# A two-layer hybrid encoder on one core: TensorE in the order in which the kernel emits its instructions

## The chip, the cores and the metric

The kernel runs on one NeuronCore of a Trainium2 chip. Its time is the device time of one execution in microseconds (us). Five engines work side by side, each through its own queue of instructions: TensorE (PE in the profile, with PEld for its weight loads), VectorE (DVE), ScalarE (ACT), GpSimd (POOL) and SyncE (SP), which issues nearly all DMA transfers. An instruction that waits holds up everything behind it on its engine.

## The reference, cut to what matters

Two layers work on 256 tokens of width 2048, all in float32. Each layer mixes (windowed attention with 8 heads beside a bidirectional mLSTM with 4 heads, both fed by one projection) and then runs an MLP:

```
h    = rms_norm(x, g_pre_mix)
proj = h @ w_in                       # 2048 -> 4624 columns
att  = window_attention(...)          # rope, |t-s| <= 128, a sink per head
mem  = mlstm_mixer(...)               # conv + silu on q/k, gates, forward and backward scans
x    = x + rms_norm(concat(att, mem) @ w_out, g_post_mix)
h    = rms_norm(x, g_pre_mlp)
u    = square(relu(h @ w_up))         # 2048 -> 8192
x    = x + rms_norm(u @ w_down, g_post_mlp)
```

## The kernel before, in words

**Weights and precision.** All weights come once, in pieces of up to 128 x 2048 values (1 MB). `load` (line 168) emits for each piece a DMA into `raw` (two buffers), a ScalarE copy to `whi` (line 191) and a VectorE subtraction to `wlo` (line 192), so that a value is a high and a low part. `whi` and `wlo` have four buffers each, and a copy may begin when TensorE has done its last matmul with the piece that held the buffer. Activations are split in the same way. Every product is three matmuls: high by high, high by low, low by high, in `mm_k` (lines 203 to 205) or in `mm_stationary` (lines 272 to 274).

**Tiles of a layer.** Ten `in` tiles of up to 512 columns (the fourth has 272), four `out` tiles, and four blocks of four `up` and four `down` tiles. In `mm_tile` (line 220) the activations are the loaded operand and a tile is 16 k steps by two halves of the tokens (t = 0, 1) by three matmuls, 96 in all. All up-tiles but a layer's first go through `mm_stationary`, where the weights are the loaded operand: 192 matmuls of 256 columns, in two pairs of two weight pieces. After each pair, `up_evac` applies Relu (line 848) and Square (849) on ScalarE to a tile `uz`, and then splits it into `uT`:

```
both = psmm.tile([P, 2, 512], F32, tag="mm", name="mms")
for pair in range(2):
    ps = both[:, pair].rearrange("p (i t) -> p i t", i=2)
    for i in range(2):
        hi, lo = pieces[key][2 * pair + i]
        ...
    after(pair, ps)
```

Results go to PSUM: pool `psmm` has two such tiles of two banks, pool `psax` four of one bank for everything else.

**Small work between the matmuls.** The attention and mLSTM work is written as generators. `mm_tile` calls `pump` (line 210) after each k step, which takes one step of the first generator in `urgent` and one in `later`. So the source itself interleaves six matmuls with a small step, and the generators hold yields (`SLACK`, three steps) between a producer and its consumer. The ones used below: `attend` (line 369: scores `sc`, probabilities `pr`, transposes `pp`, copy `pT`, product `po`), `side_kv` (transposes `pk`), `gates` (line 425: transposes `prow`, scans on VectorE, transposes `pcol` of `re`, `rwe` and `rb`), and `mlstm_head` (line 540: `st`, `dp`, `kp`, `cp`, `wp`, `pn`).

**Norms.** `pre` (line 327) makes a quarter of a normalized, transposed activation: four transposes `ptx` (line 332), a VectorE product `xg` (336), and a split into high (ScalarE, 324) and low part (325). The first tile of the program is fed in eight groups, each with its `pre` written directly ahead of its 12 matmuls. At the later boundaries `pre_at` (line 659) puts the calls between matmuls of the tiles before and after. The first up-tile ends in `up_first` (line 837: Relu, Square, transposes `ptu`).

**What sets the order.** The whole program is traced inside a tile context, whose scheduler simulates the engines. On each engine it takes the earliest-written instruction that its simulation holds to be ready, so an instruction written later may go ahead of one that has to wait. It also assigns buffers, and adds the waits. The change is in `kernel` (line 918).

## Time and profile before

| | |
|---|---|
| time, median of 3 runs | 2148.2 us (2144.47 to 2152.57) |
| the profiled execution's own time | 2145.2 us |
| its span, first to last instruction | 2143.4 us |
| mean granted TensorE clock | 0.996 of full speed |
| TensorE busy | 2100.0 us, 98% of the span |
| TensorE weight loads busy | 1855.3 us, 87% |
| VectorE busy | 1135.4 us, 53% |
| ScalarE busy | 983.9 us, 46% |
| GpSimd busy | 60.8 us, 3% |
| moved by DMA | 388.37 MB, mean 181 GB/s |

Matmuls are pipelined, so one lasts longer than the step from its start to the next one's. Where they follow each other without a wait, the step from start to start tells the pace. An engine's idle time matters only where it holds up the engine that has the most to do.

### The profile page before, as it was taken

To read this page: it belongs to the slowest core of one execution; us is meant where nothing else is said; L and a number is where in the kernel's file an instruction comes from. 1 tells how busy PE (TensorE), PEld (TensorE's weight loads), DVE (VectorE), ACT (ScalarE), POOL (GpSimd) and SP (SyncE) were. 2 spreads that over 40 slices of the span, in tenths; PEclk is the share of its full clock that TensorE was granted. 3 is DMA by queue.
4 is the path that set the end of the run, shared out by engine and by line. 5 is a ranking of instruction groups with operands and counts; after the bars stand their busy time and mean duration, and the time that the engine had idled before them with its cause. 6 is when DMAs were issued, how large, how long until landed. Compare 5 with 4: busy or idle time off the path is not lost.

```text
span 2143.4 us, 28980 instructions
## 1 busy us (share of the span) xinstructions
PE 2100.0 (98%) x12412; PEld 1855.3 (87%) x12412; DVE 1135.4 (53%) x1219; ACT 983.9 (46%) x1077; POOL 60.8 (3%) x68
## 2 busy tenths in 40 slices
PE   8999999999999999999999999999999999999998
PEld 6878887988998998898878788879889989989986
DVE  6656566544444444445567656464444444444454
ACT  5455545453443353345354555455445434533542
POOL 0000002000000000000020000030000000000000
PEclk9999999999999999999999999999999999999999
DMA  7434355555555455546444344545555555554553
GB/s 256 163 135 175 120 194 180 197 192 190 188 194 191 169 197 207 186 174 215 174 181 161 134 150 148 206 149 195 207 190 193 189 190 183 195 193 173 191 205 118
DMA packets 62209, 388.37 MB, mean 181 GB/s; under 512 B 9600, under 2 KB 10112, under 8 KB 17280
## 3 DMA queue, kind: packets, MB, share of 16 engines
q1 hardware_dynamic: 61936, 386.48, 51.4%
q8 instruction: 97, 1.59, 0.3%
q14 instruction: 32, 0.26, 0.0%
q10 hardware_dynamic: 144, 0.03, 0.0%
HBM read 384.39 MB, written 2.10 MB: 180 GB/s over the span
## 4 chain that ended last, share of the span: by engine, by line
PE 92%; DVE 2%; DMA 2%; ACT 2%; POOL 1%; issue 1%; SPq 1%; POOLq 0%; DVEq 0%; ACTq 0%
PE mm L205 19%; PE mm L204 19%; PE mm L203 19%; PE mms L272 10%; PE mms L274 10%; PE mms L273 10%; DMA raw<-wall 1%; PE sc L378 1%; PE pn L594 1%; DVE xs L792 1%; PE po L417 1%; DVE wlo L192 1%; POOL h2T L325 1%; ACT whi L191 0%; ACT uz L848 0%
## 5 line engine op out<-in xcount | busy, mean ns | idle before, releaser
L192 DVE TENSOR_TENSOR wlo<-raw,whi 128x2048 fp32r<-128x2048 f32 (+3 forms) x374 | 828.8, 2217 | 885.7 <-ACT whi L191 885.3
L191 ACT ACTIVATE whi<-raw 128x2048 fp32r<-128x2048 f32 (+3 forms) x374 | 693.9, 1855 | 922.7 <-PE mm L205 506.6
L272 PE MATMUL mms<-h2T,whi 128*128 128x256 f32 x1920 | 535.2, 279 | 7.0 <-ACT uz L848 6.8
L273 PE MATMUL mms<-h2T,whi 128*128 128x256 f32 x1920 | 533.3, 278 | 0.0
L274 PE MATMUL mms<-h2T,wlo 128*128 128x256 f32 x1920 | 530.5, 278 | 0.0
L204 PE MATMUL mm<-wlo,uT 128*128 128x512 f32 x1024 | 398.5, 389 | 0.0
L203 PE MATMUL mm<-whi,uT 128*128 128x512 f32 x1024 | 398.5, 389 | 0.0
L205 PE MATMUL mm<-whi,uT 128*128 128x512 f32 x1024 | 398.2, 389 | 0.0
L272 PEld LDWEIGHTS mms<-h2T,whi 128*128 128x128 f32 x1920 | 360.7, 188 | 11.8 <-ACT uz L848 11.1
L273 PEld LDWEIGHTS mms<-h2T,whi 128*128 128x128 f32 x1920 | 362.3, 189 | 0.3
L274 PEld LDWEIGHTS mms<-h2T,wlo 128*128 128x128 f32 x1920 | 360.0, 188 | 0.0
L203 PE MATMUL mm<-whi,hT 128*128 128x512 f32 (+2 forms) x640 | 241.9, 378 | 8.8 <-ACT hT L324 6.4
L205 PE MATMUL mm<-whi,hT 128*128 128x512 f32 (+2 forms) x640 | 241.7, 378 | 1.4 <-POOL hT L325 1.4
L204 PE MATMUL mm<-wlo,hT 128*128 128x512 f32 (+2 forms) x640 | 241.0, 377 | 0.0
L204 PEld LDWEIGHTS mm<-wlo,uT 128*128 128x128 f32 x1024 | 192.2, 188 | 39.7
L203 PEld LDWEIGHTS mm<-whi,uT 128*128 128x128 f32 x1024 | 192.2, 188 | 39.7
L205 PEld LDWEIGHTS mm<-whi,uT 128*128 128x128 f32 x1024 | 192.2, 188 | 39.4
L203 PEld LDWEIGHTS mm<-whi,hT 128*128 128x128 f32 x640 | 121.8, 190 | 29.0 <-ACT hT L324 7.0
L205 PEld LDWEIGHTS mm<-whi,hT 128*128 128x128 f32 x640 | 121.6, 190 | 22.7 <-POOL hT L325 2.2
L204 PEld LDWEIGHTS mm<-wlo,hT 128*128 128x128 f32 x640 | 121.7, 190 | 19.8
L869 DVE SCALAR_TENSOR_TENSOR A_mlp<-mm,s2q,A_mlp 128x512 f32<-128x512 f32 x48 | 34.0, 747 | 37.0 <-PE mm L205 37.0
L203 PE MATMUL mm<-whi,memT 128*128 128x512 f32 x128 | 50.5, 394 | 0.0
(221 smaller groups left out, 1460.5 us busy)
## 6 DMA issues: line engine op xcount, KB each, us to landing
raw<-wall SPq DMA_DIRECT2D x350, 1024.0 KB, 4.8
raw<-wall SPq DMA_DIRECT2D x8, 544.0 KB, 3.6
g<-gpost SPq DMA_DIRECT2D x16, 256.0 KB, 4.5
raw<-wall SPq DMA_DIRECT2D x8, 512.0 KB, 3.5
xs<-x_in SPq DMA_DIRECT2D x8, 256.0 KB, 5.2
raw<-wall SPq DMA_DIRECT2D x8, 256.0 KB, 6.1
y_out<-xs SPq DMA_DIRECT2D x8, 256.0 KB, 2.8
cossin<-rope SPq DMA_DIRECT2D x1, 256.0 KB, 7.1
```

The lines of the kernel that those rows point to most:

```text
L191: nc.scalar.activation(hi[:, sl], raw[:, sl], AF.Copy)
L192: nc.vector.tensor_tensor(out=lo[:, sl], in0=raw[:, sl], in1=hi[:, sl].bitcast(F32), op=ALU.subtract)
L203: nc.tensor.matmul(dst, lhsT=xh, rhs=hi, start=(k == 0), stop=False)
L204: nc.tensor.matmul(dst, lhsT=xh, rhs=lo, start=False, stop=False)
L205: nc.tensor.matmul(dst, lhsT=xl, rhs=hi, start=False, stop=(k == KC - 1))
L272: nc.tensor.matmul(ps[:, i], lhsT=hi[:, k], rhs=Tk[:, 0], start=(k == 0), stop=False)
L273: nc.tensor.matmul(ps[:, i], lhsT=hi[:, k], rhs=Tk[:, 1], start=False, stop=False)
L274: nc.tensor.matmul(ps[:, i], lhsT=lo[:, k], rhs=Tk[:, 0], start=False, stop=(k == KC - 1))
L325: (eng or nc.vector).tensor_tensor(out=lo, in0=ps, in1=hi.bitcast(F32), op=ALU.subtract)
L378: nc.tensor.matmul(sc[:, j], lhsT=qT[:, q0 + j, t * P:(t + 1) * P], rhs=kT[:, g], start=(j == 0), stop=False)
L417: nc.tensor.matmul(po[:, j], lhsT=vA[:, kb, g * HD:(g + 1) * HD], rhs=pT[:, kb], start=(kb == 0), stop=(kb == 1))
L869: nc.vector.scalar_tensor_tensor(out=acc[:, t, sl], in0=ps, scalar=s2[t], in1=acc[:, t, sl], op0=ALU.mult, op1=ALU.add)
```

## The change

TensorE is put under a manual schedule: its instructions keep the sequence in which the kernel's code emits them. VectorE, ScalarE, GpSimd and SyncE are still arranged by the scheduler, which simulates them against TensorE's fixed sequence. No instruction of the computation is added or removed.

```diff
     with tile.TileContext(nc, schedule_with_timeline_sim=True) as tc:
-        encoder_kernel(tc, *args)
+        with tc.manual_schedule(engines={mybir.EngineType.PE}):
+            encoder_kernel(tc, *args)
```

**Place one: the middle of a stationary up-tile, TensorE.** `mms` is the tile's PSUM, `h2T` the activations, `whi` and `wlo` the two parts of a weight piece. The names end in the numbers that the build gives them. Before, pair 0 of a tile (mms_3460) ends and the next tile (mms_3687) begins:

```order
L272 MATMUL mms_3460<-h2T1_2881,whi_3216 128x256
L273 MATMUL mms_3460<-h2T1_2881,whi_3216 128x256
L274 MATMUL mms_3460<-h2T1_2881,wlo_3217 128x256
L272 MATMUL mms_3687<-h2T0_2880,whi_3437 128x256 [waits Activation_49]
L273 MATMUL mms_3687<-h2T0_2880,whi_3437 128x256
L274 MATMUL mms_3687<-h2T0_2880,wlo_3438 128x256 [waits DVE_49]
```

and 41 matmuls later pair 1 of the first tile begins, after a wait for ScalarE:

```order
L274 MATMUL mms_3687<-h2T1_2881,wlo_3438 128x256
L272 MATMUL mms_3687<-h2T1_2881,whi_3437 128x256
L273 MATMUL mms_3687<-h2T1_2881,whi_3437 128x256
L272 MATMUL mms_3460<-h2T0_2880,whi_3222 128x256 [waits Activation_49]
L273 MATMUL mms_3460<-h2T0_2880,whi_3222 128x256
L274 MATMUL mms_3460<-h2T0_2880,wlo_3223 128x256
```

Now, at the same place (the tile is called mms_3462 here):

```order
L272 MATMUL mms_3462<-h2T1_2883,whi_3218 128x256
L273 MATMUL mms_3462<-h2T1_2883,whi_3218 128x256
L274 MATMUL mms_3462<-h2T1_2883,wlo_3219 128x256
L272 MATMUL mms_3462<-h2T0_2882,whi_3224 128x256 [waits Activation_49]
L273 MATMUL mms_3462<-h2T0_2882,whi_3224 128x256
L274 MATMUL mms_3462<-h2T0_2882,wlo_3225 128x256 [waits DVE_49]
```

Pair 1, whose first matmul waits for the Relu `uz` on pair 0, now follows pair 0 directly; the 41 matmuls of the next tile are behind it.

**The same place on ScalarE, now.** `raw` is a landed weight piece, `uz` the evacuated pair:

```order
L324 ACTIVATE uT0_2985<-uz_3433 128x2x256 [waits Activation_49]
L191 ACTIVATE whi_3439<-raw_3438 128x2048 [waits DMAHW3_49,DVE_49,PE_49]
L191 ACTIVATE whi_3445<-raw_3444 128x2048 [waits DMAHW4_49,DVE_49,PE_49]
L848 ACTIVATE uz_3559<-mms_3462 128x512 [waits PE_49,Pool_49]
L849 ACTIVATE uz_3559<-uz_3559 128x512 [waits Activation_49]
L324 ACTIVATE uT1_2986<-uz_3559 128x2x256 [waits Activation_49]
```

Before, the rows around this Relu are the same. The second of the two copies takes the buffer of the piece that pair 0 has just used. Its wait on PE is for the last-but-one matmul of pair 0, an L273, and the Relu's is for the last one, an L274.

**Place two: the start, TensorE.** `ptx` are the transposes of `pre`, `mm` the first tile. Before:

```order
L204 MATMUL mm<-wlo,hT_140 128x512
L205 MATMUL mm<-whi,hT_140 128x512
L332 MATMUL ptx<-ident,xs 128x128 x12
L203 MATMUL mm<-whi,hT_140 128x512
L204 MATMUL mm<-wlo,hT_140 128x512
L332 MATMUL ptx<-ident,xs 128x128
L205 MATMUL mm<-whi,hT_140 128x512
```

Now:

```order
L205 MATMUL mm<-whi,hT_142 128x512
L203 MATMUL mm<-whi,hT_142 128x512
L204 MATMUL mm<-wlo,hT_142 128x512
L205 MATMUL mm<-whi,hT_142 128x512
L332 MATMUL ptx<-ident,xs 128x128 x4
L203 MATMUL mm<-whi,hT_142 128x512
L204 MATMUL mm<-wlo,hT_142 128x512
```

The transposes of several groups went ahead together, between matmuls of earlier groups; now four stand directly ahead of the 12 matmuls that need them, eight times. On VectorE, the fourth to sixth group now (hT0 and hT1 are the low parts for k steps 0 to 7 and 8 to 15):

```order
L192 TENSOR_TENSOR wlo_188<-raw_184,whi_187 128x2048
L747 TENSOR_SCALAR nsink_8898<-snk_8896 128x8
L336 TENSOR_TENSOR xg_295<-ptx_290,gcol_96 128x512
L325 TENSOR_TENSOR hT0_142<-xg_295,hT0_142 128x4x128
L192 TENSOR_TENSOR wlo_203<-raw_201,whi_202 128x2048
L336 TENSOR_TENSOR xg_316<-ptx_311,gcol_96 128x512
L192 TENSOR_TENSOR wlo_209<-raw_207,whi_208 128x2048
L325 TENSOR_TENSOR hT1_143<-xg_316,hT1_143 128x4x128
L336 TENSOR_TENSOR xg_337<-ptx_332,gcol_96 128x512
```

Before, all eight `xg` stand ahead of the subtraction for the tile's fourth piece, so that of the weights only the third piece's lies among them; now five of them stand behind it or behind later ones.

**Place three: the gates, TensorE.** `pcol` holds transposes of `re`, `rwe` and `rb`, which VectorE and ScalarE make from `prow`. Before:

```order
L505 MATMUL pcol<-ident,re 128x36 x2
L535 MATMUL ptqk<-ident,qkn 128x128 x4
L203 MATMUL mm<-whi,hT_141 128x512
L204 MATMUL mm<-wlo,hT_141 128x512
L505 MATMUL pcol<-ident,rwe 128x36
L205 MATMUL mm<-whi,hT_141 128x512
```

Now:

```order
L205 MATMUL mm<-whi,hT_143 128x512
L505 MATMUL pcol<-ident,re 128x36 x2
L505 MATMUL pcol<-ident,rwe 128x36 x2
L505 MATMUL pcol<-ident,rb 128x36 x2
L203 MATMUL mm<-whi,hT_143 128x512
L204 MATMUL mm<-wlo,hT_143 128x512
```

The six transposes were spread over matmuls of the same tile and the next; now they stand together, 18 matmuls behind `prow`.

## Rows read from the trace of the kernel before

**Rows 1.** The page, part 1: engine, busy us (share of the span), instructions.

```profile
PE 2100.0 (98%) x12412; PEld 1855.3 (87%) x12412; DVE 1135.4 (53%) x1219; ACT 983.9 (46%) x1077; POOL 60.8 (3%) x68
```

**Rows 2.** Groups by line and form: count | busy us, mean ns | idle before, releasers.

```profile
L191 ACT ACTIVATE whi<-raw 128x2048 fp32r<-128x2048 f32 x350 | 671.6, 1919 | 888.0 <-PE mm L205 493.1 <-PE mms L273 255.4 <-DMA raw<-wall 118.9
```

**Rows 3.** Waits of TensorE: us in total, times, longest.

```profile
PE mms L272 <- ACT uz L848: 6.8, 15, 0.5
...
PE pp L411 <- DVE pr L400: 3.0, 4, 1.2
PE po L417 <- ACT pT L414: 2.8, 2, 2.1
```

**Rows 4.** Timeline of TensorE in up-tiles: start us, duration us, operation [idle before <-releaser].

```profile
611.40 0.39 PE L274 MATMUL mms<-h2T,wlo 128*128 128x256 f32 x2
611.62 0.28 PE L272 MATMUL mms<-h2T,whi 128*128 128x256 f32 x1
...
617.75 0.40 PE L203 MATMUL mm<-whi,uT 128*128 128x512 f32 x1
618.60 0.39 PE L272 MATMUL mms<-h2T,whi 128*128 128x256 f32 x1 [0.45 <-ACT uz L848]
```

**Rows 5.** Timeline of ScalarE, same place.

```profile
611.60 1.93 ACT L191 ACTIVATE whi<-raw 128x2048 fp32r<-128x2048 f32 x1 [3.51 <-PE mms L273]
613.43 0.58 ACT L848 ACTIVATE uz<-mms 128x512 f32<-128x512 f32 x1
...
617.95 0.60 ACT L848 ACTIVATE uz<-mms 128x512 f32<-128x512 f32 x1 [0.24 <-PE mms L274]
```

**Rows 6.** Stretches: us, busy (count) by engine, then PEclk, DMA share, GB/s.

```profile
133.70:137.00 3.30, 3.30 (x12) 2.67 (x10) 1.35 (x4) 0.81 (x2) 0.00 (x0) 0.50 0.55 179
140.50:143.90 3.40, 3.16 (x8) 2.49 (x9) 0.79 (x4) 0.18 (x1) 0.00 (x0) 0.50 0.00 0
...
372.50:376.00 3.50, 2.82 (x12) 2.01 (x12) 3.40 (x6) 2.30 (x5) 3.50 (x3) 1.00 0.00 0
...
1075.75:1079.10 3.35, 2.80 (x7) 2.22 (x8) 2.83 (x7) 3.35 (x6) 2.52 (x3) 0.50 0.68 248
```

**Rows 7.** Timeline of TensorE at three longer gaps.

```profile
132.25 0.70 PE L417 MATMUL po<-pT,scr 128*128 128x256 f32 x2 [2.10 <-ACT pT L414]
...
372.28 0.50 PE L203 MATMUL mm<-whi,h2T 128*128 128x512 f32 x1 [1.33 <-ACT h2T L324]
...
1074.87 0.50 PE L203 MATMUL mm<-whi,hT 128*128 128x512 f32 x1 [2.76 <-ACT hT L324]
```

**Rows 8.** Timeline of TensorE where tile 0 ends.

```profile
36.00 0.39 PE L204 MATMUL mm<-wlo,hT 128*128 128x512 f32 x1
36.23 0.39 PE L205 MATMUL mm<-whi,hT 128*128 128x512 f32 x1
38.52 0.41 PE L694 MATMUL pk<-ident,ra 128*128 128x128 f32 x2 [1.91 <-DVE ra L363]
```

**Rows 9.** Timeline of VectorE in tile 0.

```profile
14.60 0.69 DVE L336 TENSOR_TENSOR xg<-ptx,gcol 128x512 f32<-128x512 f32 x1
...
15.99 0.69 DVE L325 TENSOR_TENSOR hT<-xg,hT 128x512 fp32r<-128x512 f32 x1 [0.45 <-ACT hT L324]
...
27.88 2.29 DVE L192 TENSOR_TENSOR wlo<-raw,whi 128x2048 fp32r<-128x2048 f32 x1 [0.22 <-ACT whi L191]
...
34.77 2.29 DVE L192 TENSOR_TENSOR wlo<-raw,whi 128x2048 fp32r<-128x2048 f32 x1 [3.86 <-ACT whi L191]
```

**Rows 10.** Timelines of TensorE and ScalarE at the gates of layer 0.

```profile
153.72 0.60 PE L458 MATMUL prow<-ident,gpad 128*36 128x128 f32 x4
...
167.58 0.40 ACT L495 ACTIVATE rb<-rb 36x256 f32<-36x256 f32 x1
```

**Rows 11.** Timeline of VectorE at the first attention pair.

```profile
77.01 0.69 DVE L385 TENSOR_REDUCE mx<-sc 128x2 f32<-128x512 f32 x1 [0.83 <-PE sc L381]
...
79.53 0.62 DVE L400 TENSOR_SCALAR pr<-pr,rs 128x256 f32<-128x256 f32 x2
```

## The prediction

> **What bounds the kernel now.** I read the page's busy times first, then what TensorE waits for, then the timeline where it waits. TensorE is busy for 98% of a span of 2143.4 us [rows 1]. Its matmuls follow each other at a fixed pace, 0.23 us for 512 columns [rows 8] and 0.11 us for 256 columns [rows 4], so what is not pace is a wait for another engine. The view of waits puts the largest part of these, 6.8 us in 15 waits, between the stationary up-tiles and `uz`, the Relu that ScalarE applies to a finished pair, and finds 3.0 and 2.8 us at the attention's `pp` and `po` [rows 3]. So the kernel is a stream of TensorE instructions with almost nothing lost, and what the change can do is add waits or take these few away. Nearly all of that is settled by one question per place: how much TensorE work stands between a producer and its consumer, before and now.
>
> **Up-tiles, the main term.** A stationary tile is computed as two pairs, and the first matmul of pair 1 waits for the Relu on pair 0. Before, the scheduler put matmuls of the next tile in between: 41 of them in 14 of the 30 tiles, one or two in the other 16. Now nothing stands there, in all 30 (15 a layer). What ScalarE does at that point is the second half of the story: in its new sequence the copy `whi` of a weight piece stands directly ahead of the Relu in all 30 tiles, and that copy is released by the last-but-one matmul of the pair, so it always starts first. The trace of before shows this very sequence under its cover: the last matmul of a pair starts at 611.40, `whi` runs from 611.60, the Relu from 613.43 for 0.58, to 614.01 [rows 4, 5]. TensorE starts 0.05 us after a Relu ends (618.55 to 618.60 in the same rows). Uncovered, the next matmul starts at 614.06 instead of 611.51: 2.55 us lost, times 30 is **+77 us**. In exchange the short waits of before go: a matmul of 512 columns was followed after 0.85 us instead of 0.23 [rows 4], 0.62 us in about 15 places, **-9 us**. Bounds: if the Relu came first, a boundary would cost 0.58 plus the 0.2 between matmul and ScalarE's start, some 0.75 us, 22 us in all; if the piece's transfer were late as well, up to one more `whi` (1.92 us [rows 2]) each, 57 us more. I take the value of the trace, as its whole sequence is there.
>
> **The clock after such a stall.** After the idle 2.10 us at 130.1 and the 2.76 us at 1072.1, TensorE's granted clock stood at its lower level, 1.2 GHz, over stretches of 3.3 to 3.4 us [rows 6, 7]; after 1.33 us at 370.9 it stayed at 2.4 GHz [rows 6, 7]. A stretch of 3.4 us at half speed costs 1.7 us of matmuls. The new stalls leave TensorE idle for about 2.4 us (its last matmul ends 0.2 us into them), between the two that were followed by a slow stretch. Bounds 0 and 30 x 1.7 = 51 us; with two rows for it and one of half the length against it I take 18 of 30, **+31 us**. The Trainium skill's page "TensorE: Matmul & The Clock Gate" (section "Why this matters for your kernels") advises no idle gaps above about 3 us between bursts of matmuls. By that rule these stalls are short enough and this term is nothing, 31 us less in the sum; the trace's 2.10 us speaks against it.
>
> **Start of the program.** Tile 0 runs in eight groups (four pieces by two token tiles), each with its own four transposes `ptx`. Before, the scheduler sent the transposes of later groups ahead. Now a group's transposes come only after the group before it, and its matmuls wait for the whole chain `xg`, `hT`, low part: from 14.60 to 16.68, 2.1 us [rows 9]. Seven groups by 2 us are +14 us, the lower bound of this term. VectorE's new sequence makes it worse: it puts `xg` of the fourth, fifth and seventh groups behind (or their low part behind) a weight subtraction `wlo`. The fourth waits for the one at 27.88 and the fifth for those at 34.77 and after [rows 9]. With 2.29 us for a second `wlo`, the fifth group can run to its third matmul only at about 40.8 and ends at 43.3; three more of 5.3 us (0.4 transposes, 2.1 chain, 0.1, 2.7 matmuls) and one `wlo` in the seventh end tile 0 near 61.5, where before it ended at 36.2 [rows 8]: +25. The 1.91 us before `pk` go, since 24 matmuls now stand ahead of it [rows 8]. **+23 us**; the upper bound is +35, if the last four groups run at the lower clock.
>
> **Mixer stage, both layers.** `prow` to the last `pcol` is a long chain on VectorE and ScalarE: from 153.72 to 167.98, when ScalarE has finished `rb` [rows 10]. About half of those 14 us are weight copies and attention work in between. Before, some 70 matmuls covered it; now 18 do (4.1 us), and all three transposes stand together. **+8 us** (4 a layer; bounds 2 and 10 a layer). Attention: scores to probabilities take 3.1 us undisturbed [rows 11]; behind the second scores now stand 24 matmuls, 5.4 us, but 2.9 to 4.2 us where the 272-column tile runs, and one `whi` with its `wlo` (4.2 us) can come between. Between `pp` and `po` stand 6 matmuls, 1.4 or 0.7 us, for a copy of 0.6 us plus its start. I allow 2.5 us for each of 8 pairs, +20, and take off the waits of before there (3.0 + 2.8 us [rows 3]) and two slow stretches [rows 6] of 1.7 us: **+11 us** (bounds -9 and +30). The mLSTM heads come closer together (36 matmuls between `kp` and `pn`, but 6 between `pn` and the next `st`, for a chain of about 2 us): **+4 us**, bounds 0 and +14. `ptu` now stands directly behind its tile, so TensorE waits for two Relus and two Squares, each like `uz` (0.58) [rows 5]: 2.5 us a layer, **+5 us**.
>
> **Between the sub-layers** `ptx` now waits for the residual, with 18 matmuls of cover (4.1 us). In exchange the second eight transposes come 30 matmuls ahead of their use, where before TensorE stood for 1.33 to 2.76 us [rows 7]. I set this at **0**, between -9 and +9. The down-projections, the output projection's first three tiles and the transfers keep their order; their cover is TensorE's unchanged work.
>
> **Sum** on the profiled execution's 2145.2 us: 77 - 9 + 31 + 23 + 8 + 11 + 4 + 5 = +150, so **2295 us**. That execution lies 3 us under the median of the runs shown, which I leave out.
>
> **Rivals.** (1) The clock holds. For it: the 1.33 us gap. Against it: the two longer ones. 2295 - 31 = 2264 us, chance 0.2. (2) The copy isn't in the way: if its release came later than ScalarE's look at the Relu, a boundary costs 0.75 us and leaves the clock alone: 2295 - 55 - 31 = 2209 us. Against it stands every such place of the trace where the copy went first; 0.06. (3) Stalls at the upper bounds, with the clock down after nearly each: 2295 + 20 + 12 + 19 = 2346 us (clock, start, attention); in its favour, every engine but TensorE is busy half the time and collisions add up; 0.14. (4) The other side: the weight stream, not TensorE, sets the pace. If a piece's transfer took over 5.5 us, the time of its 48 matmuls, plus a quarter of the stall, then TensorE would stand at each piece anyway, the new stalls would only move that waiting, the start would wait for weights as before, and 9 us of short waits would go: 2136 us. Against it: `whi` waited for transfers for 118.9 us of its 888, and for TensorE's release of buffers for nearly all the rest [rows 2]; and no TensorE wait on weights is in the view. 0.03. That the change does nothing is excluded by the printed order.
>
> **Chances and range.** My forecast has 0.57; its own terms (start 14 to 35, attention and mLSTM -9 to +44, clock 15 to 51) spread it over 2250 to 2335. The range takes in rival 1 with its spread and most of rival 3: 2225 to 2350. Outside lie rivals 2 and 4 and a tail of rival 3, some 0.15. No change that a measurement could tell, about 0.5% or 11 us either way: faster 0.02, same 0.02, slower 0.96.
>
> **What would show it.** In the new profile: TensorE's wait on `uz` at line 272 in 30 places of about 2.4 us, some 70 us in all, with `whi` running across each; stretches at 1.2 GHz behind more than half of them; the first `pk` after 60 us; `pcol` waiting on `rb`. The prediction is wrong if the waits on `uz` are under 1 us each, or if the time per stationary tile grows by less than 2 us. It is wrong as to size if the clock stays up, or if attention's `pp` and `po` wait for over 40 us in all.

## The result, and the profile after

The changed kernel takes 2322.7 us (median of 4 runs, 2315.8 to 2332.3), the kernel before 2149.0 us (4 runs, 2144.5 to 2152.6). The ratio is 1.081, with an interval of 1.077 to 1.086: slower by 8%. The profiled execution takes 2320.2 us, 175 us over the 2145.2 us on which the forecast's sum was made; the sum had +150, 2295 us, and the range 2225 to 2350 holds the time.

The page's busy line and three of its groups, after (engine, busy us, share of the span, count; a group's count | busy, mean ns | idle before, releaser):

```profile
PE 2148.1 (93%) x12412; PEld 1892.8 (82%) x12412; DVE 1140.0 (49%) x1219; ACT 985.3 (42%) x1077; POOL 58.6 (3%) x68
...
L192 DVE TENSOR_TENSOR wlo<-raw,whi 128x2048 fp32r<-128x2048 f32 (+3 forms) x374 | 830.6, 2222 | 997.8 <-ACT whi L191 997.2
L191 ACT ACTIVATE whi<-raw 128x2048 fp32r<-128x2048 f32 (+3 forms) x374 | 693.6, 1855 | 1079.5 <-PE mm L205 579.6
L272 PE MATMUL mms<-h2T,whi 128*128 128x256 f32 x1920 | 548.3, 286 | 71.1 <-ACT uz L848 71.1
```

The other engines are as busy as before, ScalarE with 985 us (984 before); the copies `whi` cost the same 1.86 us each on average. TensorE's share falls from 98% [rows 1] to 93%: its busy time grows by 48 us (matmuls at the lower clock last longer), the span by 175. What it waits for, after (line, waited for: us in total, times, longest):

```profile
PE mms L272 <- ACT uz L848: 71.1, 30, 2.4
PE ptx L332 <- DVE xs L792: 17.4, 4, 6.9
PE mm L203 <- ACT hT L324: 17.2, 8, 3.6
PE mm L203 <- DVE part_ro L308: 11.8, 2, 5.9
PE pcol L505 <- ACT rwe L493: 9.5, 4, 2.8
PE ptu L843 <- ACT ur L840: 6.6, 4, 1.7
PE pp L411 <- DVE pr L400: 5.3, 2, 2.7
PE mm L205 <- DVE hT L325: 4.0, 4, 1.7
```

The first line stands where 6.8 us in 15 waits stood before [rows 3]. The second and the fourth had no term in the forecast: the fourth and 10.3 us of the second lie at the boundary between mixer and MLP, the other 6.9 us of the second (at 1185.41) at the boundary from layer 0's MLP to layer 1.

One middle of a stationary tile, timeline of TensorE, ScalarE and VectorE after (start us, duration us):

```profile
473.08 0.28 PE L274 MATMUL mms<-h2T,wlo 128*128 128x256 f32 x1
473.28 1.91 ACT L191 ACTIVATE whi<-raw 128x2048 fp32r<-128x2048 f32 x1 [3.73 <-PE mms L273]
475.10 0.58 ACT L848 ACTIVATE uz<-mms 128x512 f32<-128x512 f32 x1
475.22 2.29 DVE L192 TENSOR_TENSOR wlo<-raw,whi 128x2048 fp32r<-128x2048 f32 x1 [3.35 <-ACT whi L191]
475.71 0.63 ACT L849 ACTIVATE uz<-uz 128x512 f32<-128x512 f32 x1
...
475.73 0.38 PE L272 MATMUL mms<-h2T,whi 128*128 128x256 f32 x1 [2.37 <-ACT uz L848]
475.95 0.28 PE L273 MATMUL mms<-h2T,whi 128*128 128x256 f32 x1
```

This is the sequence of [rows 4, 5] without its cover: the copy starts 0.20 us after the pair's last matmul, the Relu follows it, and TensorE stands from 473.08 to 475.73, 2.65 us from start to start, 2.53 more than its step of 0.12. All 30 places show 2.53. Behind each, the next step is 0.22 us too instead of 0.11 or 0.12 (475.73 to 475.95), so that a stall costs 2.64 us in all, 79 us in 30.

Where the time went, stage by stage. The stages are cut at first matmuls: of the output projection, of the first stationary tile, and of the next layer.

| stage | before, us | after, us | difference | the forecast's terms for it |
|---|---|---|---|---|
| layer 0, to the output projection | 264.9 | 300.8 | +35.9 | 34.5 (start 23, half of gates 8, attention 11, mLSTM 4) |
| layer 0, output and first up-tile | 119.8 | 133.7 | +13.9 | 2.5 (ptu), boundary 0 |
| layer 0, stationary up and down | 690.1 | 739.6 | +49.5 | 49.5 (half of 77 - 9 + 31) |
| layer 1, to the output projection | 252.8 | 272.9 | +20.1 | 11.5 |
| layer 1, output and first up-tile | 118.8 | 134.2 | +15.5 | 2.5 (ptu), boundary 0 |
| layer 1, stationary up and down, end | 697.0 | 737.3 | +40.3 | 49.5 |

The clock, after: three stretches of the windows view (us, busy and count of TensorE, then granted clock, DMA share, GB/s):

```profile
450.50:453.90 3.40, 3.40 (x29) 1.00 0.28 67
476.70:480.10 3.40, 3.40 (x19) 0.50 0.43 120
370.80:377.60 6.80, 2.86 (x7) 0.50 0.56 209
```

The first two stand behind two equal stalls of 2.53 us; behind one the clock stayed at 2.4 GHz, behind the other it went to 1.2 GHz for 3.4 us. Read over the whole span, 27 stretches at 1.2 GHz last 132 us together, against 4 with 16 us before. Only 12 of them, 41 us, begin in the stationary tiles, each at the end of a stall or just behind it.

### The profile page after: what moved, and what is told of

The parts are those of the page before. It is cut to its first block, busy times and chain, and to the rows that moved or that the text cites. A ratio compares the mean times of both kernels' runs of the same rounds, so it can differ in the third digit from the quotient of the medians.

```text
span 2318.4 us, 28978 instructions
## 1 busy us (share of the span) xinstructions
PE 2148.1 (93%) x12412; PEld 1892.8 (82%) x12412; DVE 1140.0 (49%) x1219; ACT 985.3 (42%) x1077; POOL 58.6 (3%) x68
## 4 chain that ended last, share of the span: by engine, by line
PE 88%; ACT 5%; DVE 4%; issue 2%; DMA 1%; POOL 1%; SPq 0%; POOLq 0%; DVEq 0%; ACTq 0%
PE mm L203 18%; PE mm L205 18%; PE mm L204 18%; PE mms L272 10%; PE mms L273 10%; PE mms L274 10%; ACT whi L191 3%; DVE wlo L192 2%; DMA raw<-wall 1%; ACT uz L848 1%; PE sc L378 1%; PE po L417 1%; PE pn L594 1%; POOL h2T L325 1%; DVE xs L792 0%
## 5 line engine op out<-in xcount | busy, mean ns | idle before, releaser
L272 PE MATMUL mms<-h2T,whi 128*128 128x256 f32 x1920 | 548.3, 286 | 71.1 <-ACT uz L848 71.1
L274 PE MATMUL mms<-h2T,wlo 128*128 128x256 f32 x1920 | 544.3, 283 | 0.0
L273 PE MATMUL mms<-h2T,whi 128*128 128x256 f32 x1920 | 544.2, 283 | 0.0
L272 PEld LDWEIGHTS mms<-h2T,whi 128*128 128x128 f32 x1920 | 373.2, 194 | 77.3 <-ACT uz L848 77.1
L273 PEld LDWEIGHTS mms<-h2T,whi 128*128 128x128 f32 x1920 | 372.7, 194 | 0.2
L274 PEld LDWEIGHTS mms<-h2T,wlo 128*128 128x128 f32 x1920 | 371.5, 194 | 0.0
L203 PE MATMUL mm<-whi,hT 128*128 128x512 f32 (+2 forms) x640 | 251.5, 393 | 18.1 <-ACT hT L324 17.2
L205 PE MATMUL mm<-whi,hT 128*128 128x512 f32 (+2 forms) x640 | 242.6, 379 | 4.0 <-DVE hT L325 4.0
L203 PEld LDWEIGHTS mm<-whi,hT 128*128 128x128 f32 x640 | 124.2, 194 | 39.9 <-ACT hT L324 19.4
L205 PEld LDWEIGHTS mm<-whi,hT 128*128 128x128 f32 x640 | 123.9, 194 | 29.6 <-DVE hT L325 7.7
L203 PE MATMUL mm<-whi,attT 128*128 128x512 f32 x128 | 52.2, 408 | 11.8 <-DVE part_ro L308 11.8
```

The costliest lines, as they stand in the source:

```text
L203: nc.tensor.matmul(dst, lhsT=xh, rhs=hi, start=(k == 0), stop=False)
L205: nc.tensor.matmul(dst, lhsT=xl, rhs=hi, start=False, stop=(k == KC - 1))
L272: nc.tensor.matmul(ps[:, i], lhsT=hi[:, k], rhs=Tk[:, 0], start=(k == 0), stop=False)
L273: nc.tensor.matmul(ps[:, i], lhsT=hi[:, k], rhs=Tk[:, 1], start=False, stop=False)
L274: nc.tensor.matmul(ps[:, i], lhsT=lo[:, k], rhs=Tk[:, 0], start=False, stop=(k == KC - 1))
```

## The experiments

**A PSUM tile for each pair.** The wait at the middle of a stationary tile is a buffer's: pair 1 writes the second half of the tile whose first half the Relu still reads.

```diff
-        both = psmm.tile([P, 2, 512], F32, tag="mm", name="mms")
         for pair in range(2):
+            both = psmm.tile([P, 2, 512], F32, tag="mm", name="mms")
             ps = both[:, pair].rearrange("p (i t) -> p i t", i=2)
```

> The changed kernel (profiled 2320 us), but each pair of a stationary tile has a PSUM tile of its own, so that pair 1 no longer has to wait for the Relu on pair 0; TensorE's sequence stays as emitted. Theory A (the wait is a buffer dependence, and each of the 30 costs the 2.53 us seen between two matmuls, plus half-clock stretches behind about 12 of them): 30 x 2.53 - 30 x 0.11 = 73 us and 12 x 1.7 = 20 us go, so about 2227 us; no L272 wait on the Relu above 0.3 us is left. Rival B (the weight pieces or ScalarE set the pace there, and the Relu is only where the waiting shows): the stall moves to another wait, and the time stays above 2290 us. Rival C (the clock falls for another reason than these stalls): 73 us go, but the time at 1.2 GHz inside the up-tiles stays at about 40 us: 2247 us.

Measured: 2238.6 us (2236.4 to 2239.8, 4 runs). No wait on the Relu is left, and no stretch at 1.2 GHz begins in the stationary tiles (12 in the changed kernel). The up and down stages fall by 49.0 and 38.8 us, to 690.6 and 698.5, which is what they took before the change. So theory A holds for the cause and for the clock, and B and C fall. But 88 us are 5 less than the 93 expected, and that number took the pace off a second time: with 79 us for the stalls and 20 for the clock it should have been 99, so 11 are missing. (Another 5 are lost in the input stages, which the edit doesn't touch.) Something takes part of the gain in the up-tiles back, and it shows in the count of matmuls in windows of equal length (us, busy and count, clock, DMA share, GB/s), first in this kernel:

```profile
592.00:606.00 14.00, 14.00 (x121) 1.00 0.52 184
640.00:654.00 14.00, 14.00 (x121) 1.00 0.56 197
462.00:476.00 14.00, 14.00 (x126) 1.00 0.47 169
```

and in the kernel before:

```profile
545.00:559.00 14.00, 14.00 (x122) 1.00 0.61 215
590.00:604.00 14.00, 14.00 (x126) 1.00 0.60 212
```

At the full clock and without a gap, TensorE starts either 121 to 122 or 126 matmuls of 256 columns in 14 us. Whole tiles take 22.61 or 21.76 us, 0.118 or 0.113 us a matmul. By the steps from matmul to matmul, 24 of the 30 tiles run at the slower pace here, and the equivalent of about 12 in the kernel before as in the changed one: 12 tiles by 0.85 us are 10 us, the size of what is missing. The traffic of the DMAs does not tell the two paces apart: 215 and 212 GB/s before. Three later kernels come back to this.

**Four one-bank PSUM buffers for all matmul results**, so that the fourth output tile meets older banks:

```diff
-    psmm = ctx.enter_context(tc.tile_pool(name="psmm", bufs=2, space=bass.MemoryType.PSUM))
+    psmm = ctx.enter_context(tc.tile_pool(name="psmm", bufs=4, space=bass.MemoryType.PSUM))
...
-            ps = [psmm.tile([P, NT, 512], F32, tag="mm", name="mm")[:, 0] for _ in range(NT)]
+            ps = [psmm.tile([P, 512], F32, tag="mm", name="mm") for _ in range(NT)]
...
+            ps = psmm.tile([P, 512], F32, tag="mm", name="mms").rearrange("p (i t) -> p i t", i=2)
```

> As the kernel with a PSUM tile per pair, but all matmul results go to four one-bank PSUM buffers instead of two of two banks, so that the output projection's fourth tile starts in the banks of the second tile, not of the third. Theory A (the 6.0 us ahead of the fourth output tile in each layer are the wait for the evacuation of the third, whose last step is VectorE's product behind a weight subtraction): 12 us less than the kernel with a tile per pair, and about 7 us more if the half-clock stretches of 6.8 us behind those two waits go: about 2210 us. Rival B (that tile waits for the norm's partial sum itself, or for the residual): no difference to the kernel with a tile per pair, about 2227 us, the wait of 6 us still there.

Measured: 2229.9 us (2226.2 to 2231.6), 8.7 less than with a tile per pair. What stood there in the changed kernel (timeline, all engines):

```profile
368.21 1.91 ACT L191 ACTIVATE whi<-raw 128x2048 fp32r<-128x2048 f32 x1 [3.52 <-PE mm L205]
...
368.47 0.39 PE L205 MATMUL mm<-whi,attT 128*128 128x512 f32 x1
370.03 0.58 ACT L313 ACTIVATE junk<-mm 128x512 bf16<-128x512 f32 x1
370.16 2.29 DVE L192 TENSOR_TENSOR wlo<-raw,whi 128x2048 fp32r<-128x2048 f32 x1 [3.14 <-ACT whi L191]
...
372.43 0.68 DVE L808 TENSOR_TENSOR A_out<-mm,g 128x512 f32<-128x512 f32 x1
...
373.21 0.60 ACT L313 ACTIVATE junk<-mm 128x512 bf16<-128x512 f32 x1 [2.51 <-DVE part_ro L308]
...
374.00 0.68 DVE L808 TENSOR_TENSOR A_out<-mm,g 128x512 f32<-128x512 f32 x1
374.60 0.14 DVE L308 TENSOR_SCALAR part_ro<-part_ro 128x1 f32<-128x1 f32 x1
...
374.74 0.79 PE L203 MATMUL mm<-whi,attT 128*128 128x512 f32 x1 [5.88 <-DVE part_ro L308]
```

The fourth output tile has a PSUM buffer for each token half. Its first three matmuls go to the first half; the fourth, in emitted order, goes to the second half, whose buffer the third tile's results have just filled. They are read through a chain on two engines, in which the piece's copy and its subtraction stand ahead, and the last reader (L808 at 374.00, not the `part_ro` that the view names) ends 0.06 us before TensorE starts. Before, the scheduler ran all 48 matmuls of the first half in front of the second. With the one-bank buffers both output stages take 90.8 us instead of 98.4 and 99.0, and the wait is gone, as theory A has it, for 16 us. Only half of that reaches the total, which stays 20 us above the expected 2210: the first input stage is 9.9 us longer, with attention's waits on `pr` at 12.8 us instead of 5.3. TensorE's order is the same there, so the likely maker is the sequence that the scheduler then chose for the other engines; no run took this apart.

**The Relu ahead of the copies.** The PSUM dependence stays, but the next tile's pieces are loaded behind the Relu:

```diff
-        load(pos[key] + 1)
...
-            after(pair, ps)
+            load(pos[key] + 1, only=2 * pair + 2, behind=after(pair, ps).ins)
...
+                with tc.issue_after(behind) if behind is not None else nullcontext(): nc.scalar.activation(hi[:, sl], raw[:, sl], AF.Copy)
```

> The changed kernel with the PSUM dependence kept, but ScalarE's order altered: the weight copies of the next tile are issued behind the Relu of each pair, never ahead of it. Theory A (the copy of 1.9 us ahead of the Relu makes up most of the stall): a boundary costs about 0.75 us beyond the pace instead of 2.4, so 30 x 1.7 = 50 us go, and with a stall that short the clock stays up, 20 us more: about 2250 us. Rival B (the Relu is late for another reason, or the copy, once behind, makes the weights late): the boundaries stay above 2 us or a wait on the weights appears, 2300 us or more.

Measured: 2246.2 us (2243.2 to 2252.6). One boundary (timeline of TensorE and ScalarE) and the view of waits:

```profile
603.60 0.28 PE L274 MATMUL mms<-h2T,wlo 128*128 128x256 f32 x1
603.91 0.60 ACT L848 ACTIVATE uz<-mms 128x512 f32<-128x512 f32 x1 [8.24 <-PE mms L274]
604.41 1.91 ACT L191 ACTIVATE whi<-raw 128x2048 fp32r<-128x2048 f32 x1
...
604.56 0.39 PE L272 MATMUL mms<-h2T,whi 128*128 128x256 f32 x1 [0.69 <-ACT uz L848]
```

```profile
PE mms L272 <- ACT uz L848: 21.0, 30, 0.7
```

The boundary costs 0.96 us from start to start, 0.85 over the pace (1.02 and 0.91 in six places, the first block of each layer), where the forecast's rival 2 had 0.75. All 30 waits are left, each at 0.7 us, and no stretch at 1.2 GHz follows any of them. So the copy made 1.7 of the 2.53 us, and with the stall cut to a third the clock no longer fell behind it. Theory A holds. Some 8 us of the gain come from the pace: the equivalent of 3 tiles, not 12, runs at 22.61 us here.

**The one-bank buffers in the kernel before.** The edit of the four one-bank buffers, with TensorE left to the scheduler.

> The kernel before (scheduled TensorE, 2149 us) with the four one-bank PSUM buffers. Theory A (the scheduler's reordering already hides this dependence but for 15 short waits): 9 us or less are gained in the up-tiles and 0 to 4 at the boundaries, 2136 to 2149 us. Rival B (the dependence costs the scheduled kernel nothing that another wait does not take over): 2149 us, no change. Slower, above 2155 us, would mean that finer buffers let the scheduler choose a worse sequence.

Measured: 2144.9 us (2141.9 to 2146.3, 10 runs) against 2146.9 us (13 runs), ratio 0.9988 with an interval of 0.9977 to 1.0000. All waits on the Relu are gone, 15 of some 0.75 us beyond the pace (0.5 to 0.7, and 0.11 in the step behind), 11 us, and nearly nothing is gained: 27 of the 30 tiles now run at 22.61 us, where before it was the equivalent of 12, and 15 tiles by 0.85 us are 13 us. The outcome is rival B's, through a mechanism that no theory had.

**The emitted order in the mixer alone, and in the MLP alone.** The scheduler keeps the rest:

```diff
-        big = apool.tile([P, 4112], F32, tag="A", name="A_mix")
+        big = apool.tile([P, 4112], F32, tag="A", name="A_mix"); m = tc.manual_schedule(engines={mybir.EngineType.PE}); m.__enter__()
...
+        m.__exit__(None, None, None)
```

(mixer: the region ends behind the fourth output tile; MLP: it begins there and ends with the layer)

> The kernel before, with TensorE's emitted order kept only in the projection, attention, mLSTM and output tiles of both layers; the MLP is left to the scheduler. Theory A (the cost of the change adds up by stages, and these stages make the difference seen between the two traces: 36 and 20 us in the input tiles, 5 and 8 in the output tiles, 0 to 16 around the first up-tiles): +69 to +85 us, 2216 to 2232 us. Theory B (the forecast's own terms: start 23, gates 8, attention 11, mLSTM 4, some clock): +46 to +60 us, about 2200 us. Rival C (the stages depend on each other, a stall in one only takes up slack of another): under +40 us.

> The kernel before, with TensorE's emitted order kept only in the MLP (up and down tiles) of both layers. Theory A (additive by stages: 50 and 40 us in the up and down tiles, 0 to 16 around the first up-tiles): +90 to +106 us, 2237 to 2253 us, with the waits on the Relu in 30 places of 2.4 us. Theory B (the forecast's terms: 77 - 9 + 31 + 5 = 104): 2251 us, the clock at 1.2 GHz behind 18 of the 30 stalls. Rival C (not additive): outside 2230 to 2260 us.

Measured: 2222.8 us (2219.8 to 2223.5) for the mixer, +74.7 on the 2148.1 us of the kernel before; 2252.3 us (2238.9 to 2255.3) for the MLP, +104.2. The sum, +178.9, is within 5 us of the whole change's +174.6. So the costs add up, theory A in both; C falls. Stage by stage the fit is looser than in the total: the two profiles' differences together miss those of the changed kernel by up to 8.5 us a stage. The first of these misses, 7.5 us, is the start: in the mixer's kernel the first tile ends at 71 us, in the changed one at 63. In the MLP the forecast's own terms, 104 us, are met as well, but not one by one: the waits on the Relu are the same 71.1 us in 30, 14 of them followed by a stretch at 1.2 GHz (18 forecast), and 19 us of the difference lie around the first up-tiles, where the forecast had 5. In the mixer the forecast's terms (theory B) are too small.

**The start.** The first tile's groups of transposes are emitted one to two groups ahead of their matmuls:

```diff
-    for q in range(NPC):
-        in_stage[1][0, PK * q] = lambda q=q: pre(0, q, hT, 0, nc.vector)
-        in_stage[1][1, PK * q] = lambda q=q: pre(1, q, hT, 0, nc.vector)
+    for j, key in enumerate([(0, 0), (0, 1), (0, 3)] + [(i % 2, PK * (i // 2) + 1) for i in range(1, 6)]):
+        in_stage[1][key] = lambda j=j: pre(j % 2, j // 2, hT, 0, nc.vector)
```

> The changed kernel with the first tile's groups of transposes emitted one to two groups ahead of their matmuls, nothing else. Theory A (the start loses its time because each group's transposes, product and split stand directly ahead of the matmuls that need them): the first tile ends near 40 us instead of 63, the time falls by 20 us or more, to about 2300 us. Rival B (VectorE's sequence, with the weight subtractions ahead of the products, or the arrival of x and weights sets the start): less than 8 us go, 2315 us.

Measured: 2292.9 us (2291.6 to 2297.0), 29.7 less than the changed kernel. The stage to the output projection falls from 300.8 to 281.0 us; `pk`, which began at 38.5 us before [rows 8] and at 68.5 us in the changed kernel, begins at 48.7 us. The first tile ends at 42 us (near 40 expected). So 20 us of the start were missing cover, which is theory A. The two profiled executions differ by 23 us: layer 0's MLP, which the edit doesn't touch, takes 8 us less, with 6 instead of 8 stalls followed by a stretch at 1.2 GHz and fewer tiles at the slower pace, and layer 1's input stage 3.5 us more. The other 6 us lie in the spread of the runs. Which stalls and which tiles these are is not fixed by TensorE's order, which is the same there.

**Breaks and the pace, first try.** In the kernel before, a PSUM tile for each pair, except in each block's first stationary tile:

```diff
+        shared = key[3] == (1 if key[2] == 0 else 0)
         for pair in range(2):
+            if pair == 0 or not shared: both = psmm.tile([P, 2, 512], F32, tag="mm", name="mms")
```

> The kernel before with a PSUM tile per pair in the stationary tiles, but the two pairs of each block's first stationary tile still share one, so that one short wait on the Relu is left at the head of each block. Theory P (the 256-column matmuls run at one of two paces, 0.113 or 0.118 us, that is 21.76 or 22.61 us a tile; a seamless stream keeps the pace it entered with, 0.118 behind a down-tile, and a short break sets it to 0.113): behind the wait the rest of each block runs at 21.76 us, some 25 x 0.85 = 21 us less than the kernel with four one-bank buffers, less 8 x 0.6 us for the waits: about 2128 us. Rival Q (the pace follows the stretch of the program, or the buffers' banks, and not the break): tiles of 22.61 us remain and the time stays at 2143 to 2149 us.

Measured: 2146.5 us (2141.1 to 2151.1, 12 runs), ratio 0.9993 with an interval of 0.9983 to 1.0004. The number expected is missed, since the break was not made: in six of the eight blocks the scheduler put the next tile's matmuls into the wait and no gap was left; all four tiles of those six run at 22.61 us. In the other two, the first blocks of the layers, the faster pace is there before the gap: it begins where four transposes `ptu`, 0.36 us, stand between the first tile's matmuls. So this kernel says nothing for or against a break on the Relu.

**Breaks and the pace, second try.** The same PSUM tiles, but the stationary tiles of a block keep their emitted order, so that nothing can fill the break, and the Relu goes ahead of the copies:

```diff
+                    if n < 2 and not (b and n): m = tc.manual_schedule(engines={mybir.EngineType.PE}); m.__enter__()
                     mm_stationary(key, h2T, up_evac)
+                    if n == 3: m.__exit__(None, None, None)
```

> The kernel before, but the stationary tiles of each block keep TensorE's emitted order, each pair has its own PSUM tile except in the block's first stationary tile, and the weight copies are issued behind the Relu. So one break of about 0.75 us stands at the head of each of the eight blocks, and nowhere else in them. Theory P (two paces, 0.113 and 0.118 us for 256 columns; a short break sets the faster one and a seamless stream keeps it): behind the break all tiles of a block run at 21.76 us; the up-tiles take 30 x 21.76 + 8 x (0.75 + 0.43) = 662 us where the kernel with four one-bank buffers took 675 and the kernel before 668: about 2132 us, 0.6% under the kernel before. Rival Q (the pace belongs to the stretch of the program or the buffers): 22.61 us a tile in the later blocks in spite of the break, 2148 us or more.

Measured: 2134.4 us (2131.5 to 2135.6, 5 runs) against 2147.6 us (9 runs): ratio 0.9931, interval 0.9918 to 0.9943. It beats both kernels. Waits, and windows of the second to fourth tile of one block, behind its break at 549.60:

```profile
PE mms L272 <- ACT uz L848: 5.7, 8, 0.7
```

```profile
563.00:577.00 14.00, 14.00 (x126) 1.00 0.41 152
585.00:599.00 14.00, 14.00 (x126) 1.00 0.40 151
606.00:620.00 14.00, 14.00 (x126) 1.00 0.39 151
```

The stationary tiles take 662.9 us together (662 expected), against 674.8 with seamless one-bank buffers and 668.0 before. In the six blocks that follow a down-tile, the half tile in front of the break runs at 0.118 us and everything behind it at 0.113; in the two first blocks of a layer the pace changes at `ptu` already, so that their break buys nothing. Theory P's time and its tiles came as expected, against Q: the later blocks, at 22.61 us in two kernels without a break, run at 21.76 us behind one. Compared with the seamless kernel, 12 us are gained with 7 us of breaks paid.

As a general rule, though, theory P fails on a kernel that was already measured, the one with the emitted order in the mixer alone. In its MLP the matmuls stand in the same groups as in the kernel before. Where pair 1 of a stationary tile follows a matmul of a down-tile, the wait of 0.45 us and the step of 0.85 are the same in both (669.28 to 670.13 there, 617.75 to 618.60 in [rows 4]). Behind it the mixer's kernel runs at the slower pace and the kernel before at the faster one (windows, in this order):

```profile
671.00:681.00 10.00, 10.00 (x87) 1.00 0.63 229
619.00:629.00 10.00, 10.00 (x90) 1.00 0.65 247
```

In the mixer's kernel 10 of the 16 short waits in the stationary tiles were followed by the slower pace, 7 of them although the matmuls ahead had the faster one; in the kernel before it was 1 of 15. So the pace can change at a break, but which one follows hangs on something that no run here isolates.

**Cover written into the emitted order.** The changed kernel with one-bank buffers, the start as above, and:

```diff
-        yield
-        yield
-        yield
+        for _ in range(9): yield
         pc = psax.tile([P, 6, NG], F32, tag="ax", name="pcol")
...
+                while i and held: held.pop(0)()
                 hi, lo = pieces[key][2 * pair + i]
```

(`held` keeps the transposes and the split of `up_first` for the middle of the next tile's first pair)

> The changed kernel with four one-bank PSUM buffers (2230 us alone), the first tile's transposes emitted ahead (30 us in the changed kernel alone), nine steps instead of three between the gates' scans and pcol (54 matmuls of cover instead of 18), and the transposes of the first up-tile emitted in the middle of the next tile. Theory A (each of these waits is a producer with too few matmuls written behind it, and cover takes it away): 2230 - 30 for the start, - 12 and up to 7 of clock at the gates, - 6.6 and up to 6 of clock at the first up-tiles: about 2172 us, without waits on rwe, rb and ur. Rival B (a wait taken away at one place comes back at the next, since the chains behind are late too): the input stages get shorter by less than half of that, and the time stays above 2190 us.

Measured: 2177.6 us (2176.8 to 2178.1), 52 us less than with the one-bank buffers alone. The waits on `rwe`, `rb` and `ur` are gone. The input stages fall by 34.7 and 6.4 us, the stages of the first up-tile by 5.5 and 4.6. Theory A holds. Of what is left, 30 us over the kernel before, the largest waits are the residual's four (17.3 us), attention's on `pr` (12.8 us) and the mLSTM's at `cp` (5.2 us).

## Why the prediction was right, and where its steps were not

**The up-tiles: right.** The term was 30 x 2.55 = 77 us; the trace shows 30 x 2.53 = 76. It is a buffer's wait, and 1.7 us of each is the copy ahead of the Relu, as the order showed; the experiments confirm the buffer (a PSUM tile for each pair) and the copy (the Relu ahead). The 0.11 us in the step behind each stall, 3 us in all, had no term.

**The 15 short waits, -9: incomplete.** They went, and were worth 11 us, but they also did something: in six of the eight blocks the first such break put the matmuls behind it on the faster pace. The forecast took 0.11 us as the pace of all 256-column matmuls; it is 0.113 or 0.118. In the sum this did nothing, since the changed kernel has the equivalent of 12 slower tiles as well; that was luck.

**The clock, +31: right in kind, wrong in place.** In the stationary tiles 12 of 30 stalls, and not more than half, were followed by a stretch at 1.2 GHz, 12 x 1.7 = 20 us; in two other kernels with the same 30 stalls it was 14 and 10. That makes 36 of 90 stalls of 2.53 us followed by the lower clock, and none of 30 stalls of 0.85. The Trainium skill's page "TensorE: Matmul & The Clock Gate" (section "Why this matters for your kernels") advises no idle gaps above about 3 us between bursts of matmuls; the traces differ, in that gaps shorter than that were followed by the lower clock too. The step that was mis-sized is that the term was counted for the up-tiles alone: 91 of the 132 us at 1.2 GHz lie elsewhere, at the start, attention, the gates and the boundaries, and these were in no term of the sum (only the start's upper bound named them). They are worth at most 45 us, 8 of which the kernel before had as well, and less where TensorE waited anyway, as in the window from 370.80, where it was busy for 2.86 of 6.80 us.

**The start, +23: right.** Tile 0 ends at about 63 us (61.5 forecast), and the cover written in takes 20 us off.

**The mixer's other terms.** Gates +8: the waits on `rwe` and `rb` are 13 us, the chain outlasting its 18 matmuls of cover by more than the 4 us a layer that the term had. Attention +11, over-sized: `pp` waits 5.3 us and `po` is not in the view, where before they waited 5.8 together [rows 3]. With other buffers the wait was 12.8 us, so the bounds were fair. mLSTM +4: the waits at `cp` and `kp` are 6.4 us. `ptu` +5: 6.6 us.

**Between the sub-layers, 0: the step that failed.** The two stages with output projection and first up-tile grew by 29.4 us, of which `ptu` was foreseen. The prediction said that "the output projection's first three tiles and the transfers keep their order; their cover is TensorE's unchanged work". That is so for the three tiles, but the fourth was passed over: its sequence changed from all of the first half ahead of the second to an alternation, and 2 x 5.9 us came of it. Nearly as much, 2 x 5.15 us, is the residual, and its third wait, 6.9 us, falls into layer 1's input stage. The forecast set 18 matmuls of cover, 4.1 us, against it, and let what was missing cancel with the waits of before. No experiment touched the residual; its cause is read from the trace. The timeline after shows what its chain holds (VectorE, and TensorE's transposes):

```profile
405.30 0.16 DVE L302 TENSOR_TENSOR r_ro<-y_ro,a_ro 128x1 f32<-128x1 f32 x1
405.41 2.29 DVE L192 TENSOR_TENSOR wlo<-raw,whi 128x2048 fp32r<-128x2048 f32 x1
407.62 2.73 DVE L792 SCALAR_TENSOR_TENSOR xs<-A_out,r_ro,xs 128x512 f32<-128x512 f32 x4
...
408.51 1.09 PE L332 MATMUL ptx<-ident,xs 128*128 128x128 f32 x4 [5.15 <-DVE xs L792]
```

The scale `r_ro` was ready at 405.46 and the first residual began at 407.62: a weight subtraction had slipped in. The same collision, a copy or a subtraction of 1.9 to 2.3 us ahead of a short step that TensorE waits for, was priced at the up-tiles and at the start, and forgotten here.

**The sum.** The stationary tiles' three terms had 99 us and the stages show 90, which the trace nearly fills with 79 for the stalls, -11 and 20 for the clock; the input stages had 46 and show 56; the boundaries 5 and 29. The first two misses cancel, by luck, so the difference of 25 us between +150 and +175 is the boundaries' nearly by itself. Rival 3, all stalls at their upper bounds at 2346 us, lies about as near to the time as the forecast (23 and 28 us off), but not by its mechanism: its terms were the clock in the up-tiles, the start and attention, and none of them came to its bound. Rival 1 falls with the clock's rows, rival 2 with the timeline after, where the copy runs ahead of the Relu, and the third experiment, rival 4 with the first: without the stalls the up-tiles ran at TensorE's pace, and no wait for weights took their place.

## What to carry to other kernels

When an engine's order is fixed, list every buffer that it writes again and every product of another engine that it reads, and count for each the work that stands in between in the new order; then look which long step on the other engine can slip in ahead, since that step, not the short one named in the source, made most of the stall here. A false dependence of two halves of one PSUM tile cost next to nothing here as long as the scheduler filled it (2 us of 2147), and 2.5 us each time as soon as it couldn't: it is better taken out of the program than out of the order. With that dependence left only in each block's first stationary tile, the copies behind the Relu and the order fixed in the stationary tiles alone, the kernel gained 0.7%; fixed everywhere, as it stood, it lost 8%.

## What the runs showed of the hardware that was not expected

A seamless stream of 256-column matmuls, with a weight load for each, runs at 22.61 or at 21.76 us for 192 of them, at the same granted clock of 2.4 GHz. Behind a down-tile without a gap it was always the slower pace. Behind breaks of 0.85 to 0.91 us it was the faster one in all six such blocks of the kernel with eight breaks, and with the Relu ahead of the copies it stayed the faster one over all later breaks. Behind stalls of 2.53 us both paces occur, and behind waits that cost 0.5 to 0.7 us in two kernels too (the faster behind 14 of 15 in the kernel before, behind 6 of 16 in the mixer's kernel). Once set, a pace lasted to the next break or the next stretch at 1.2 GHz. What makes the difference was not isolated and stays open.

Equal stalls of 2.53 us at equal places were followed by 1.2 GHz in some cases and not in others, and not in the same places from one kernel to another; that is also the likely reason why the changed kernel's runs spread over 16 us (their mean granted clock from 0.965 to 0.972, the longest run with the lowest) and those of the kernel before over 8 us.
